# A two-layer diffusion backbone on one core: side streams that take a step of their own before they claim banks or wait in TensorE's queue, and head tiles that leave PSUM inside their loop

## The chip, the cores and the metric

The kernel runs on one core of a Trainium2 chip. The metric is the device time of one execution in microseconds (us). A core has five engines that work at the same time, each through its own list of instructions in a fixed order: PE (TensorE, matrix products; PEld is its loading of weights), DVE (VectorE), ACT (ScalarE), POOL (GpSimd) and SP (which issues DMAs). An instruction that waits for a semaphore holds up everything behind it on its engine. PE writes to PSUM, of which there are eight banks; DVE and ACT read the results out.

## The reference

Two request groups, 128 context tokens and 512 latent tokens, go through two layers that share their weights. A layer norms and modulates its input (model width 1024), projects it to the inputs of four branches and to their gates, runs the branches, gates them, merges them and adds the result to the stream. Cut to what matters here:

```python
kk = kk * lax.rsqrt(jnp.sum(kk * kk, axis=-1, keepdims=True) + 1e-12)
for d, rev in ((0, False), (1, True)):            # RWKV-7 scan, forward and reverse
    w_log = -jax.nn.softplus(-(lp['rw_w0'][d] + wd_t @ lp['rw_w_up'][d])) - 0.5
    decay = heads(jnp.exp(-jnp.exp(w_log)))
    a = heads(jax.nn.sigmoid(lp['rw_a0'][d] + adf @ lp['rw_a_up'][d]))
    k_d = k_h * (1.0 + (a - 1.0) * k_a)
    s_fin, o = wkv_scan(s_init[:, d], r_h, decay, k_d, v_h, kk, a, rev)
    o_sum = o_sum + o
mu = jnp.mean(o_sum, axis=-1, keepdims=True)      # group norm of the scan's output, per head
var = jnp.mean(jnp.square(o_sum - mu), axis=-1, keepdims=True)
on = ((o_sum - mu) * lax.rsqrt(var + GN_EPS)).reshape(B, L, BR_W)
y = on * lp['rw_ln_g'] + lp['rw_ln_b'] + bonus

def rmsnorm(x, g):                                # before each layer and at the end
    return x * lax.rsqrt(jnp.mean(x * x, axis=-1, keepdims=True) + NORM_EPS) * g
```

The other branches are windowed attention with a sink, a mix of tokens within chunks, and a pooling branch. All five outputs (two streams, new keys, new values, new scan states) are float32.

## The kernel before

The 640 tokens stand in the free dimension as two halves of 320 (`HF`); the 1024 channels are eight tiles of 128 partitions (`KT`). Every large product is split into three: activations and weights are kept as a high and a low part in the type fp32r, and PE computes hi times whi, lo times whi and hi times wlo (`m<-hi,whi`, `m<-lo,whi`, `m<-hi,wlo` in the rows below). ACT casts the high part of a weight (`whi<-raw`), DVE subtracts it to get the low part (`wlo<-raw,whi`). There are 7008 such main products of 128x128 by 128x320, 3504 in each layer.

A planner (class `Clock`, from L91) writes the order of each engine once, when the program is built. It runs the main stream, which is the large products, and several **side streams**: attention (`at`), the scan of the RWKV branch, its group norm (`gn0`, `gn1`), the norm of the next layer's input (`normed`) and smaller ones. Each stream is a Python generator. A `yield` in a side stream ends a step: at that point the planner can lay main products between this step and the next, and it looks at its own model of engine times, and from a stream's second step on at its model of PSUM banks, to decide when the next step is due. A `yield` in the main stream with a name waits until a side stream has marked that name. What is written without a `yield` between stands back to back in PE's order, whatever the data behind it does at run time.

PSUM's banks are shared out by name: four `m` banks for main products, two `x` banks for most side products, one `c` and one `o` bank for attention and scan. A bank can be written again when its last result has been read.

Places in the code that the change touches:

- `rstd_thin` (L600) computes the factor of a norm. Six thin products (`x<-cst,t` and `x<-cst,nacc`: two partial sums of squares, three token blocks) go into one `x` bank, ACT takes the square root, DVE the reciprocal (`rst`), and `spread()` transposes the factors over the partitions (`x<-cst,rst`). `normed` (L622) calls both back to back for each half at the end of layer 0.
- `scan` has `decay(d)` (L709 on), whose last products `x<-cst,A` are read by four exponentials on ACT (`A<-x`). For the reverse direction (d = 1) the next step is the **value flip**: the tokens of the values are put in reverse order by a product (`x<-vn,cst`). It writes the banks that those exponentials read.
- `group_norm` (L981) starts with the **centering**: it claims two `x` banks at once and subtracts the head's mean by a product (`x<-yb,cst`).
- `head()` (L1315) computes the first six tiles of layer 0, three tiles in two halves (`ck`, `cv` and a query tile), with the sum over k outermost, into four `m` banks and the `c` and `o` banks. After the loop all six are copied out by `put`, alternately by ACT and DVE, and `put` of a second half marks the tile as ready for attention.

Of the kernel before, what the change touches and what calls it, by code (L numbers as in the profile page):

```python
# [14 lines left out]
P = 128  # L15
NL = 2
D = 1024
KT = D // P
# [3 lines left out]
HF = T // 2  # L22
# [5 lines left out]
HEAD = ["ck", "cv", "q0", "q1"]  # L28
# [267 lines left out]
def hybrid_layers_kernel(ctx: ExitStack, tc: tile.TileContext, xt, cond, condb, wm, wt, wa, wb, wo, pa, pb, pc, gfin, kctx, vctx,  # L296
# [16 lines left out]
    def X():  # L313
        return ck.alloc("x", ps_x.tile([P, 512], F32, tag="x", name="x"), 2)
# [284 lines left out]
    def rstd_thin(acc, more=None):  # L599

        ms = X()
        parts = [acc] if more is None else [acc, more]
        for i, o in enumerate((0, P, HF - P)):
            for x in parts:
                mm(ms[:, 2 * i:2 * i + 2], x[:, o:o + P], K("mean")[:, 0:2], start=i == 0 and x is acc,
                   stop=i == 2 and x is parts[-1])
        st = S([P, 6], "rst", 2)
        A.activation(st, ms[:, 0:6], AF.Sqrt, bias=eps[:, 0:1])
        V.reciprocal(st, st)

        def spread():
            bc = X()
            for i, (o, c) in enumerate(((0, 0), (P, 0), (2 * P, C))):
                mm(bc[:, o:min(o + P, HF)], st[:, 2 * i:2 * i + 1].to_broadcast([P, P]), K("ident")[:, c:P])
            A.copy(acc, bc[:, 0:HF])
            return bc

        return spread

    def normed(xs, accs, l, out, bs, ahead, more=None):  # L620
        rs = {}
        for b in bs:  # L622
            rs[b] = accs[b]
            if l:
                rstd_thin(accs[b], more)()
        for b in bs:
            out[b] = (S([P, KT, HF], f"hi{b}", dt=F32R), S([P, KT, HF], f"lo{b}", dt=F32R))
            ck.mark(f"hh{l}{b}")
        late = []

        def finish(k, ts):
            shift = mods[l][0]
            for b in bs:
                hi, lo = out[b]
                for s, e, g in segs[b]:
                    V.scalar_tensor_tensor(lo[:, k, s:e], ts[b][:, s:e], shift[:, k, g:g + 1], hi[:, k, s:e],
                                           ALU.add, ALU.subtract)
                ck.mark(f"h{l}{b}.{k}")

        for k in range(KT):  # L640
            yield f"mod{l}.{k}"
            shift, gsc = mods[l][0], mods[l][1]
            ts = {b: S([P, HF], "t", 4) for b in bs}
            for b in bs:
                for s, e, g in segs[b]:
                    V.scalar_tensor_tensor(ts[b][:, s:e], xs[b][:, k, s:e], gsc[:, k, g:g + 1], rs[b][:, s:e],
                                           ALU.mult, ALU.mult)
            if ahead and late:
                finish(*late.pop(0))
            for b in bs:  # L650
                for s, e, g in segs[b]:
                    A.activation(out[b][0][:, k, s:e], ts[b][:, s:e], AF.Identity, bias=shift[:, k, g:g + 1])
            late.append((k, ts))
            if not ahead:
                finish(*late.pop(0))
            if k + 1 < KT:
                yield VQ
        for x in late:
            finish(*x)
# [11 lines left out]
    def layer(l, h, prb):  # L671
# [23 lines left out]
        def scan(ft, ta, kt, rt, vt):  # L695
# [89 lines left out]
            for d in range(2):  # L785
                for c0, n in ((0, 8), (8, 2)):
                    px = X()
                    for hh in range(2):
                        r = slice(64 * hh, 64 * hh + 64)
                        if d:  # L790
                            mm(px[r, 0:n * C], K("anti")[r, r], vn[hh][r, c0:c0 + n, :].rearrange("p c s -> p (c s)"))
                            continue
                        for i in range(n):
                            mm(px[r, i * C:(i + 1) * C], vt[r, (c0 + i) * C:(c0 + i + 1) * C], K("ident")[r, r])
                    for hh in range(2):
                        r = slice(64 * hh, 64 * hh + 64)
                        src = px[r, 0:n * C].rearrange("p (c s) -> p c s", s=C)
                        o0 = 2 * NC - c0 - n if d else c0
                        A.copy(vn[hh][r, o0:o0 + n, :], src[:, ::-1, :] if d else src)
                yield  # L800
                yield from keys(d)
                if d == 0:
                    yield from decay(1)
            yield
            for b in range(2):
                px = X()
# [95 lines left out]
            for j in range(8):  # L902
# [12 lines left out]
                for n in lanes:  # L915
                    s = state[n]
                    for d, i in enumerate(at[n]):
                        o = slice(col[n, d], col[n, d] + C)
# [9 lines left out]
                for n in lanes:  # L928
                    for d, i in enumerate(at[n]):
                        o = slice(col[n, d], col[n, d] + C)  # L930
# [50 lines left out]
                state.update(nxt_state)  # L981
                yield
            def group_norm():
                oc = [X(), X()]
                cen = S([P, 2, HF], "v")
                sqs = []
                for b in range(2):
                    mm(oc[b][:, 0:HF], K("cent"), osum[:, hs[b]])
                    V.tensor_copy(cen[:, b], oc[b][:, 0:HF])
                    sq = S([P, HF], "t", 4)  # L990
                    A.activation(sq, oc[b][:, 0:HF], AF.Square)
                    sqs.append(sq)
                yield
                for b in range(2):
                    vr = X()
                    mm(vr[:, 0:HF], K("bones"), sqs[b])
                    rn = S([P, HF], "t", 4)
                    A.activation(rn, vr[:, 0:HF], AF.Sqrt, bias=eps[:, 2:3], scale=1.0 / 64)
                    V.reciprocal(rn, rn)
                    V.scalar_tensor_tensor(cen[:, b], cen[:, b], prm("lng")[:, ft:ft + 1], rn, ALU.mult, ALU.mult)  # L1000
                    V.scalar_tensor_tensor(osum[:, hs[b]], cen[:, b], prm("lnb")[:, ft:ft + 1], bon[:, hs[b]], ALU.add, ALU.add)
                yield
# [312 lines left out]
        def head():  # L1315
# [17 lines left out]
            if l == 0:  # L1333
# [5 lines left out]
                for k in range(KT):  # L1339
                    turn = k % 4 == 3  # L1340
                    for b, i in [(b, i) for i in range(3) for b in range(2)] if turn else [
                            (b, i) for b in range(2) for i in range(3)]:
                        yield f"h{l}{b}.{k}"
                        yield from accum([out[i][b]], ws[i], k % 4, 1, [rhs_h[b]], k, k == 0, k == KT - 1)
                        if turn and b:
                            if k + 1 < KT:
                                ws[i] = piece(0)
                            else:
                                split(nxt[2] + i)
                yield f"n{l}0"  # L1350
                for i in range(3):
                    for b in range(2):
                        put(HEAD[i], b, out[i][b])
                o = yield from main()
                for b in range(2):
                    put(HEAD[3], b, o[b])
# [331 lines left out]
```

## Time and profile before

| | us |
|---|---|
| median of 3 runs | 1394.77 |
| lowest and highest | 1393.83, 1397.92 |
| the profiled execution's own time | 1396.28 |
| its span in the profile | 1394.2 |
| PE busy | 1349.6 (97%) |
| PEld busy | 1259.7 (90%) |
| DVE busy | 925.8 (66%) |
| ACT busy | 565.3 (41%) |
| POOL busy | 48.0 (3%) |

The profile is of one execution. A timeline gives one row to each run of equal instructions: start, length from the first start to the last end, engine, line, operation, tiles, count, and in brackets how long the engine stood idle just before and what released it. Line 331 (`mm`) and 335 (transposes) are helpers for every PE instruction, line 290 for every instruction of the other engines, so instructions are told apart by their tiles. Products overlap: one main product is shown as 0.31 us long while the next starts 0.15 us after it. PEclk is the granted clock of PE as a share of full speed; its mean over the execution was 0.992.

### The profile page before, as it was taken

To read this page: it belongs to the slowest core of one execution; us is meant where nothing else is said; L and a number is where in the kernel's file an instruction comes from. 1 tells how busy PE (TensorE), PEld (TensorE's weight loads), DVE (VectorE), ACT (ScalarE), POOL (GpSimd) and SP (SyncE) were. 2 spreads that over 40 slices of the span, in tenths; PEclk is the share of its full clock that TensorE was granted. 3 is DMA by queue.
4 is the path that set the end of the run, shared out by engine and by line. 5 is a ranking of instruction groups with operands and counts; after the bars stand their busy time and mean duration, and the time that the engine had idled before them with its cause. 6 is when DMAs were issued, how large, how long until landed. Compare 5 with 4: busy or idle time off the path is not lost. (4 is left out here: it accounts for less than half of the span.)

```text
span 1394.2 us, 27698 instructions
## 1 busy us (share of the span) xinstructions
PE 1349.6 (97%) x11350; PEld 1259.7 (90%) x11350; DVE 925.8 (66%) x2056; ACT 565.3 (41%) x1258; POOL 48.0 (3%) x43
## 2 busy tenths in 40 slices
PE   5899999999999999999999999999999999999997
PEld 4889889988999988999999988898799998899997
DVE  5766677856777856658876667694377684464474
ACT  5455622234522333325555555223354233332364
POOL 0100010000000000000001001000000000000000
PEclk9999999999999999999999999999999999999998
DMA  9411133421224331751113212433022323144012
GB/s 376 148 54 61 39 108 106 108 81 66 67 88 115 106 94 63 267 187 61 61 62 120 72 54 66 109 87 88 24 60 65 89 83 82 37 157 156 22 39 76
DMA packets 86503, 132.61 MB, mean 95 GB/s; under 512 B 44744, under 2 KB 46152, under 8 KB 84456
## 3 DMA queue, kind: packets, MB, share of 16 engines
q1 hardware_dynamic: 86376, 130.84, 29.9%
q8 instruction: 89, 1.46, 0.4%
q14 instruction: 38, 0.31, 0.1%
HBM read 120.46 MB, written 10.35 MB: 94 GB/s over the span
## 5 line engine op out<-in xcount | busy, mean ns | idle before, releaser
L331 PE MATMUL m<-hi,whi 128*128 128x320 f32 x2064 | 666.1, 323 | 3.3 <-ACT whi L290 1.6
L331 PE MATMUL m<-hi,wlo 128*128 128x320 f32 x2064 | 641.4, 311 | 1.9 <-DVE wlo L290 1.9
L331 PE MATMUL m<-lo,whi 128*128 128x320 f32 x2064 | 640.6, 310 | 2.0 <-DVE lo L290 1.3
L331 PEld LDWEIGHTS m<-hi,whi 128*128 128x128 f32 x2064 | 389.9, 189 | 25.3 <-issue 10.2
L331 PEld LDWEIGHTS m<-lo,whi 128*128 128x128 f32 x2064 | 390.1, 189 | 5.1 <-DVE lo L290 2.0
L331 PEld LDWEIGHTS m<-hi,wlo 128*128 128x128 f32 x2064 | 389.5, 189 | 4.5 <-DVE wlo L290 4.2
L290 ACT CAST whi<-raw 128x640 fp32r<-128x640 f32 (+1 forms) x220 | 148.9, 682 | 282.3 <-PE m L331 262.6
L290 DVE TENSOR_TENSOR wlo<-raw,whi 128x640 fp32r<-128x640 f32 (+1 forms) x220 | 168.1, 769 | 107.6 <-ACT whi L290 104.8
L290 ACT ACTIVATE t<-m 128x320 f32<-128x320 f32 x152 | 64.2, 434 | 87.3 <-PE m L331 87.1
L290 DVE TENSOR_TENSOR kb<-kb 80x31 f32<-80x31 f32 (+15 forms) x248 | 86.2, 348 | 10.2 <-DMA kb<-ad 3.5
L290 DVE SCALAR_TENSOR_TENSOR t<-t,m 128x320 f32<-128x320 f32 x120 | 57.7, 481 | 47.0 <-PE m L331 38.0
L331 PE MATMUL m<-ysh,whi 128*128 128x320 f32 x256 | 82.6, 323 | 0.7 <-DVE t L290 0.7
L290 DVE CUSTOM_DVE_ANT_0 junk<-wt,sil 128x1024 bf16<-128x1024 f32 x64 | 79.2, 1237 | 3.8 <-DMA wt<-wt 3.6
L331 PE MATMUL m<-ysh,wlo 128*128 128x320 f32 x256 | 79.1, 309 | 0.0
L331 PE MATMUL m<-ysl,whi 128*128 128x320 f32 x256 | 79.0, 309 | 0.0
L290 DVE TENSOR_TENSOR xm<-xm,t 128x320 f32<-128x320 f32 x96 | 50.8, 530 | 3.3
L331 PEld LDWEIGHTS m<-ysh,whi 128*128 128x128 f32 x256 | 48.1, 188 | 3.4 <-DVE t L290 0.9
L331 PEld LDWEIGHTS m<-ysl,whi 128*128 128x128 f32 x256 | 48.2, 188 | 0.2
L331 PEld LDWEIGHTS m<-ysh,wlo 128*128 128x128 f32 x256 | 48.1, 188 | 0.0
L290 DVE RECIPROCAL t<-t 128x320 f32<-128x320 f32 x16 | 34.4, 2149 | 19.1 <-ACT t L290 19.1
L290 ACT ACTIVATE vn<-c 64x128 f32<-64x128 f32 x40 | 10.8, 271 | 79.0 <-DVE vn L290 79.0
L290 DVE TENSOR_TENSOR A<-x,cst 128x512 f32<-128x512 f32 x40 | 25.7, 684 | 20.6 <-PE x L331 20.6
(242 smaller groups left out, 1517.8 us busy)
## 6 DMA issues: line engine op xcount, KB each, us to landing
raw<-wb SPq DMA_DIRECT2D x128, 320.0 KB, 2.9
raw<-wa SPq DMA_DIRECT2D x92, 256.0 KB, 2.9
wt<-wt SPq DMA_DIRECT2D x32, 512.0 KB, 4.0
A<-wm SPq DMA_DIRECT2D x4, 1024.0 KB, 9.1
A<-wo SPq DMA_DIRECT2D x8, 512.0 KB, 6.0
xm<-xt SPq DMA_DIRECT2D x4, 640.0 KB
ad<-A SPq DMA_DIRECT2D x8, 320.0 KB
qr<-wm SPq DMA_DIRECT2D x2, 1024.0 KB
```

Source lines behind the costliest of these rows:

```text
L290: return f(out, *a, **k)
L331: PE.matmul(out, lhsT, rhs, start=start, stop=stop)
```

## The change

Four side steps are cut in two by a `yield`, so that main products can be laid between. In `normed` it stands between the factor of a norm and its spreading; in `scan` between the decay of the reverse direction and the value flip; in `group_norm` before the centering, which thus becomes the stream's second step, at which the planner looks at the banks. In `rstd_thin` the loops are exchanged: the three products of the first sum come first, then the three of the second. In `head()` each of the six tiles is copied out as soon as its last product is issued, within the loop, and no longer after it. No instruction is added or dropped; the planner lays all streams anew.

```diff
@@ rstd_thin
-        for i, o in enumerate((0, P, HF - P)):
-            for x in parts:
+        for x in parts:
+            for i, o in enumerate((0, P, HF - P)):
                 mm(ms[:, 2 * i:2 * i + 2], x[:, o:o + P], K("mean")[:, 0:2], start=i == 0 and x is acc,
                    stop=i == 2 and x is parts[-1])
@@ normed
             if l:
-                rstd_thin(accs[b], more)()
+                spread = rstd_thin(accs[b], more)
+                yield
+                spread()
@@ scan
                 if d == 0:
                     yield from decay(1)
+                    yield
@@ group_norm
             def group_norm():
+                yield
                 oc = [X(), X()]
@@ head
                         yield from accum([out[i][b]], ws[i], k % 4, 1, [rhs_h[b]], k, k == 0, k == KT - 1)
+                        if k == KT - 1:
+                            yield f"n{l}0"
+                            put(HEAD[i], b, out[i][b])
                         if turn and b:
...
-                yield f"n{l}0"
-                for i in range(3):
-                    for b in range(2):
-                        put(HEAD[i], b, out[i][b])
```

DVE's order at the end of the head tiles of layer 0, before. `xm0` holds the key and query tiles, `bon` the value tile, `m_267` and `m_269` are the banks of their second halves; STREAM_SHUFFLE and the two operations on `vn0` and `xm0` turn the key tile by its rotary angles, of which POOL computes one product in between:

```order
L290 TENSOR_TENSOR wlo_610<-raw_482,whi_609 128x512
L290 TENSOR_SCALAR wt_517<-wt_517 128x1024
L290 TENSOR_TENSOR sil_515<-wt_517,sil_515 128x1024
L290 TENSOR_TENSOR wlo_625<-raw_510,whi_624 128x512
L290 TENSOR_TENSOR wlo_637<-raw_525,whi_636 128x512
L290 COPY xm0_642<-m_267 128x320
L290 COPY bon_223<-m_269 128x320
L290 COPY xm0_642<-o_271 128x320
L290 STREAM_SHUFFLE vn0_578<-xm0_642 128x512
L290 TENSOR_TENSOR vn0_578<-vn0_578,xm1_574 128x512
L290 TENSOR_TENSOR xm0_642<-xm0_642,vn0_578 128x512
```

The same rows of DVE after:

```order
L290 COPY xm0_606<-m_267 128x320
L290 TENSOR_TENSOR wlo_614<-raw_482,whi_613 128x512
L290 TENSOR_SCALAR wt_517<-wt_517 128x1024
L290 TENSOR_TENSOR sil_515<-wt_517,sil_515 128x1024
L290 STREAM_SHUFFLE vn0_578<-xm0_606 128x512
L290 TENSOR_TENSOR vn0_578<-vn0_578,xm1_574 128x512
L290 TENSOR_TENSOR xm0_606<-xm0_606,vn0_578 128x512
L290 COPY bon_223<-m_269 128x320
L290 TENSOR_TENSOR wlo_636<-raw_510,whi_635 128x512
L290 COPY xm0_606<-o_271 128x320
L290 TENSOR_TENSOR wlo_650<-raw_525,whi_649 128x512
```

The copy of the key tile moves ahead of a weight split, the rotation of the key tile moves ahead of the copy of the value tile `bon`, and two weight splits move behind it.

PE's order at the value flip of layer 1, before. `x<-cst,A` are the last products of the decay, `x<-vn,cst` the flip, `o<-cst,kbt` and `c<-cst,kbt` transposes of attention's weights:

```order
L335 MATMUL o<-cst,kbt 128x128 x4
L335 MATMUL c<-cst,kbt 128x128 x4
L331 MATMUL x<-cst,A_8445 128x128 x5
L331 MATMUL x<-vn_8446,cst 64x512
L331 MATMUL x<-vn_8447,cst 64x512
L331 MATMUL x<-vn_8446,cst 64x128
L331 MATMUL x<-vn_8447,cst 64x128
L335 MATMUL o<-cst,kbt 128x128 x2
L331 MATMUL m<-hi_7571,whi 128x320
L331 MATMUL m<-lo_7572,whi 128x320
```

The end of the same stretch after. `x<-cst,A` stands twelve main products ahead of the first transpose shown here:

```order
L331 MATMUL m<-hi_7580,whi 128x320
L331 MATMUL m<-lo_7581,whi 128x320
L331 MATMUL m<-hi_7580,wlo 128x320
L335 MATMUL o<-cst,kbt 128x128 x2
L331 MATMUL m<-hi_7971,whi 128x320
L331 MATMUL m<-lo_7972,whi 128x320
L331 MATMUL m<-hi_7971,wlo 128x320
L331 MATMUL x<-vn_8455,cst 64x512
L331 MATMUL x<-vn_8456,cst 64x512
L331 MATMUL x<-vn_8455,cst 64x128
L331 MATMUL x<-vn_8456,cst 64x128
```

The flip no longer follows `x<-cst,A` directly: fifteen main products and two transposes stand between. The centering moves in the same manner, fifteen main products behind the `x<-adt,pb` that it followed, and the spreading of the factors six main products behind the thin products.

PE's order at the end of attention in layer 1, before. `o<-y,xm` is the last product of values with the transposed weights:

```order
L335 MATMUL o<-cst,kbt 128x128 x4
L335 MATMUL c<-cst,kbt 128x128 x4
L331 MATMUL m<-hi_7571,whi 128x320
L331 MATMUL m<-lo_7572,whi 128x320
L331 MATMUL m<-hi_7571,wlo 128x320
L331 MATMUL m<-hi_7953,whi 128x320
L331 MATMUL m<-lo_7954,whi 128x320
L331 MATMUL m<-hi_7953,wlo 128x320
L331 MATMUL m<-hi_7571,whi 128x320
L331 MATMUL m<-lo_7572,whi 128x320
L331 MATMUL m<-hi_7571,wlo 128x320
L331 MATMUL o<-y,xm_8152 64x128 x8
```

And after:

```order
L331 MATMUL m<-lo_7972,whi 128x320
L331 MATMUL m<-hi_7971,wlo 128x320
L335 MATMUL o<-cst,kbt 128x128 x4
L335 MATMUL c<-cst,kbt 128x128 x4
L331 MATMUL o<-y,xm_8157 64x128 x8
L331 MATMUL m<-hi_7580,whi 128x320
```

Here nine main products that stood between the transposes and the last product of values are gone from that place; the three rows follow one another.

## Rows read from the trace of the kernel before

**Rows 1.** The page, section 1: busy time and share of the span by engine.

```profile
PE 1349.6 (97%) x11350; PEld 1259.7 (90%) x11350; DVE 925.8 (66%) x2056; ACT 565.3 (41%) x1258; POOL 48.0 (3%) x43
```

**Rows 2.** Waits of PE: engine line waited for: total, times, longest.

```profile
PE x L331 <- DVE nacc L290: 12.0, 2, 10.9
PE x L331 <- ACT A L290: 4.9, 6, 1.4
PE x L331 <- DVE rst L290: 2.5, 4, 0.7
```

**Rows 3.** Timeline of PE, value flip in layer 1: start, length, instruction, [idle before].

```profile
845.83 1.28 PE L331 MATMUL x<-cst,A 128*128 128x128 f32 x10
848.50 1.41 PE L331 MATMUL x<-vn,cst 64*64 64x512 f32 x8 [1.39 <-ACT A L290]
```

**Rows 4.** Timeline of ACT over the same flip.

```profile
848.03 1.40 ACT L290 ACTIVATE A<-x 128x128 f32<-128x128 f32 x4
849.63 1.72 ACT L290 COPY vn<-x 64x512 f32<-64x512 f32 x4 [0.20 <-PE x L331]
```

**Rows 5.** Timeline of PE, first centering of layer 1.

```profile
1003.23 1.34 PE L331 MATMUL x<-adt,pb 64*128 64x320 f32 x4
1004.65 0.81 PE L331 MATMUL x<-yb,cst 128*128 128x320 f32 x2
1006.35 1.32 PE L331 MATMUL x<-yb,cst 128*128 128x320 f32 x2 [0.89 <-ACT A L290]
1007.00 0.94 PE L331 MATMUL m<-hi,whi 128*128 128x320 f32 x1
```

**Rows 6.** Timeline of PE, second centering of layer 1.

```profile
1213.28 1.24 PE L331 MATMUL x<-yb,cst 128*128 128x320 f32 x4
1214.12 0.55 PE L331 MATMUL m<-ysh,whi 128*128 128x320 f32 x1
```

**Rows 7.** Timeline of PE, the spreading of both halves' factors before layer 1.

```profile
678.74 0.88 PE L331 MATMUL x<-cst,rst 128*128 128x128 f32 x6 [0.58 <-DVE rst L290]
...
711.56 0.85 PE L331 MATMUL x<-cst,rst 128*128 128x128 f32 x6 [0.68 <-DVE rst L290]
```

**Rows 8.** Stretches: us, each engine's busy time, PEclk, DMA share, GB/s.

```profile
712.96:716.36 3.40, 3.40 (x15) 3.40 (x14) 1.64 (x4) 1.56 (x4) 0.00 (x0) 0.50 0.74 258
1006.50:1009.90 3.40, 3.40 (x12) 3.01 (x13) 0.49 (x1) 3.02 (x5) 0.00 (x0) 0.50 0.00 0
```

**Rows 9.** Timeline of PE and of DVE, head tiles of layer 0.

```profile
59.57 0.41 PE L331 MATMUL m<-hi,whi 128*128 128x320 f32 x1 [1.44 <-ACT xm L290]
...
62.21 0.55 PE L335 MATMUL x<-cst,bon 128*128 128x128 f32 x3 [0.84 <-DVE bon L290]
...
60.06 1.29 DVE L290 TENSOR_TENSOR wlo<-raw,whi 128x512 fp32r<-128x512 f32 x2
...
61.67 0.48 DVE L290 COPY bon<-m 128x320 f32<-128x320 f32 x1
...
62.47 0.74 DVE L290 STREAM_SHUFFLE vn<-xm 128x512 f32<-128x512 f32 x1
...
65.13 0.69 DVE L290 TENSOR_TENSOR xm<-xm,vn 128x512 f32<-128x512 f32 x1 [1.19 <-POOL xm L290]
...
65.75 0.74 DVE L290 STREAM_SHUFFLE vn<-xm 128x512 f32<-128x512 f32 x1
```

**Rows 10.** Timeline of DVE and of PE, end of attention in layer 1.

```profile
854.39 0.69 DVE L290 COPY y<-c 128x512 f32<-128x512 f32 x1 [0.24 <-PE c L335]
...
854.11 0.39 PE L331 MATMUL m<-hi,whi 128*128 128x320 f32 x1
854.33 0.31 PE L331 MATMUL m<-lo,whi 128*128 128x320 f32 x1
854.48 0.31 PE L331 MATMUL m<-hi,wlo 128*128 128x320 f32 x1
```

**Rows 11.** Timeline of PE, a bank taken back in the third merge of layer 1.

```profile
1225.06 0.41 PE L331 MATMUL m<-ysh,whi 128*128 128x320 f32 x1 [0.66 <-DVE t L290]
```

## The prediction

> **What bounds the kernel now.** I read the page's busy times first, then the waits of PE, then the timeline of PE around each place that the diff names, with ACT or DVE beside it, and last the granted clock in stretches. PE is busy for 97% of the span [rows 1], so a microsecond that another engine saves counts only where PE stands still for it. The waits say where: 12.0 us for `nacc`, of which 10.9 us is one wait at the start that the change does not reach; 4.9 us for `A` in six waits; 2.5 us for `rst` in four, of which two belong to the final norm and stay [rows 2]. The change can therefore win single waits of about 1 us and no more. The question is how many, what each costs besides the idle time shown, and what new waits the new order makes.
>
> Idle time understates a wait. Main products are 0.31 us long and start 0.15 us apart [rows 10], so the last one before a wait runs out for 0.16 us in which the next would already have started. I add 0.16 us to each wait that goes.
>
> [...] By the idle times alone the sum below would be some 2.5 us smaller.
>
> **The value flip.** In the first scan of layer 1 the products `x<-cst,A` start at 845.83 and the flip at 848.50, after 1.39 us idle [rows 3]. It waits for exponentials on ACT that read its banks and that run at 848.03, behind the softmax's exponentials [rows 4]. Layer 0 shows the same 1.39 us, and the second scans 0.17 us each; with the two centerings below these make the 4.9 us in six waits: 2 x 1.39 + 2 x 0.17 + 2 x 0.89 [rows 2]. The new order puts 36, 15, 12 and 12 main products between (layer 0, layer 1, then the second scans). Fifteen are 15 x 0.15 = 2.25 us, more than 1.39 + 0.16 = 1.55. So the waits go: 2 x 1.55 + 2 x 0.33 = 3.8 us. The centering below, where both ends can be read, costs 0.2 to 0.45 us more than idle plus 0.16; with 0.45 on the two long waits it would be 4.7. I take 4.3, between the two, with 3.1 (idle alone) and 4.7 as bounds. In layer 1 the attention step behind the flip needs the flip's banks, which ACT empties with four copies of 1.72 us together [rows 4]; main products cover most of that, and I charge 0.25 us.
>
> **The centering.** It waits 0.89 us in layer 1, for the last exponentials of the decay, which read the two banks that it claims [rows 5]; layer 0 shows the same 0.89 us. From `x<-adt,pb` at 1003.23 to the next main product at 1007.00 are 3.77 us [rows 5]. The products before the centering take 1.42 us of it (1003.23 to 1004.65), and a centering that does not wait takes 0.84 us from its start to the next main product [rows 6]. So the wait costs 3.77 - 1.42 - 0.84 = 1.5 us in layer 1 and by the same reckoning 1.25 us in layer 0. The new order puts fifteen main products (2.25 us) between: -2.8 us. Bounds: -1.8 (idle alone) and -3.4.
>
> **The factors.** The spreading waits 0.58 us for the first half and 0.68 us for the second [rows 7]. The new order puts six main products between, 6 x 0.15 = 0.9 us, more than 0.58 + 0.16 = 0.74 or 0.84. Both waits go: -1.6 us, bounds -1.3 (idle alone) and -1.8. The exchanged order of the thin products costs and gives nothing, since PE waits for none of their results but `rst`, which comes after the last of them in either order.
>
> **The clock.** [...] In 712.96 to 716.36 PE starts only 15 products in 3.40 us, in 1006.50 to 1009.90 only 12 [rows 8]; 3.40 / 0.15 would be 23. Each stretch loses about 8 to 11 products, 1.2 to 1.6 us. They begin 1.4 us after the wait for the second factors ends at 711.56 [rows 7] and 0.15 us after that of the centering ends at 1006.35 [rows 5], both waits that this change removes. If they follow from those waits they go: -2.8 us. But side products of few columns stand there as well and stay. I give it one half: -1.4 us, bounds 0 and -2.8.
>
> **The head tiles of layer 0.** Today main products wait 1.44 us at 59.57 for ACT to empty the first `m` bank, and the transposes of `bon` wait 0.84 us at 62.21 for DVE's copy [rows 9]. With the copies in the loop the first bank is free in time: -1.6 us. The second wait grows. DVE's copy of `bon` now stands behind the key tile's rotation, which lasts from 62.47 to 65.75, 3.28 us, with DVE held up for 1.19 us by POOL [rows 9]. The new order has on DVE one weight split, the two modulation operations, then that rotation, then `bon`. Today the two modulation operations end at 60.06, when the next split starts [rows 9]. So `bon` starts at 60.06 + 3.28 = 63.34 and ends, 0.48 us later, at 63.8. Today PE is ready for the waiting transposes at 62.21 - 0.84 = 61.4. They come fifteen main products later now, and 1.6 us are saved ahead: 61.4 + 2.25 - 1.6 = 62.0. So they wait 1.8 us, 1.0 us more than today. Sum: -0.6 us, bounds -2.4 (both waits go, if the copy comes earlier than I reckon) and +1.5 (the first wait stays, the second grows).
>
> [...] The trace of before kept the full clock here with a wait of 0.84 us. [...]
>
> **What is late next.** At the end of attention in layer 1 the last product of values now follows its transposes directly. Today the second transposes run until main products start at 854.11, and DVE's copy of them takes from 854.39 to 855.08 [rows 10]; nine main products cover that. Uncovered it is up to 855.08 - 854.11 = 0.97 us; I take +0.7, bounds +0.4 and +1.0. In the third merge of layer 1 a main product waits 0.66 us for a bank that DVE empties behind the group norm's reciprocals [rows 11]; the group norm falls elsewhere now: -0.4, bounds -0.9 and +0.7. In layer 0 nearly every side step between the head tiles and the first merge stands at another place, and over the whole program PE's order has eleven runs of side products more. New small waits are as likely there as the going of old ones, and each new run is one more place for them. By the nearest row, 0.66 us [rows 11], one or two of them are +1.0; bounds -1 and +3.
>
> **Sum.** -4.3 + 0.25 - 2.8 - 1.6 - 1.4 - 0.6 + 0.7 - 0.4 + 1.0 = -9.15 us. The profiled execution took 1396.28 us (its span is 1394.2, the rest lies around it and stays), so 1387.1. The median shown is 1.51 us below that execution: 1385.6.
>
> **Rivals.** 0.3% of this time, 4.2 us, is about what a measurement can tell from no change: faster means below 1390.6, slower above 1399.0.
>
> *The waits only change place.* The flip and the centering stop waiting, but their banks are then held longer, so that attention and the mix, which use the same two `x` banks, wait instead; the head tiles cost +1.5 and the small waits +3. For it: ACT is the releaser in most places, and its queue holds the same work. Against it: ACT is busy for less than half of the span. It leaves -4.3 + 0.25 - 2.8 - 1.6 + 1.5 + 0.7 + 3 = -2.95, and about 1 us more for the waits of attention and mix, -1.95: 1392.8.
>
> *Only the drained waits count.* The idle time of the flip, the centering and the factors goes (3.1 + 1.8 + 1.3 = 6.2 us), the clock falls where it fell, and the rest adds 0.25 + 0.7 + 1.0 - 0.4 - 0.6 = 0.95: -5.25, 1389.5. For it: at the second scans PE's waits are small and it is not seen what they cost beyond their idle time.
>
> *The clock falls at the head tiles too.* All terms as in the sum, but the two stretches of [rows 8] stay (+1.4) and the wait of 1.8 us before the transposes, longer than any that they follow, brings a third (+1.4): -6.35, 1388.4.
>
> *The second scan of layer 1 comes too late (slower).* The planner puts the second centering of layer 1 48 main products (7.2 us) later than before. From it to the third merge's bank the chain takes 1213.28 to 1225.06, 11.8 us [rows 6, 11], and in the new order 132 main products, 19.8 us, stand between it and the first product that needs its result. If the scan's own chain on DVE and ACT runs later than planned, the first 8.0 us are free and each microsecond beyond them is a microsecond of idle PE. It must be 8.0 + 9.15 = 17.2 us late to eat the gain and 21.4 us to be slower by 4.2: 1399.0. Against it: the list of waits shows no wait of more than 1.4 us after the start [rows 2], so the plan has been kept well.
>
> *More comes back.* Both clock stretches go and the head tiles lose both waits: -9.15 - 1.4 - 1.8 = -12.35, 1382.4.
>
> **How the numbers follow.** Forecast 0.48, only the drained waits 0.12, clock at the head tiles 0.10, waits change place 0.18, second scan late 0.06, more comes back 0.06. Faster holds the forecast, the two rivals below 1390.6 and the last: 0.76, of which I move 0.02 to "same" since 1389.5 lies near the edge: 0.74. Same 0.20, slower 0.06. The range 1381.0 to 1393.5 takes in all but the late scan and the outer ends of the others.
>
> **What would show it.** Right: no idle time of PE in front of `x<-vn,cst`, the first `x<-yb,cst` of each layer and the `x<-cst,rst` between the layers; no wait for `xm` at the first product after the head tiles; a wait of about 1.8 us for `bon` there; a new wait of 0.4 to 1 us before the last `o<-y,xm` of attention in layer 1; one or two stretches at half clock fewer. Wrong: a wait for `bon` under 1 us or over 3; a wait of over 1 us at a product that had none; half clock after the head tiles; or a sum of PE's waits lower by 6 us with a time that has not moved.

## The result and the profile after

The changed kernel takes 1388.47 us (median of 5 runs, 1383.34 to 1389.26); before, in 5 runs of the same series, it was 1396.31 us (1393.83 to 1397.92). The ratio is 0.994 with a 95% interval of 0.9919 to 0.9962: faster by 0.4 to 0.8%. The forecast was 1385.6 us in a range of 1381.0 to 1393.5. The profiled execution took 1388.71 us against 1396.28, 7.6 us less, where the sum had said 9.15. By the interval the gain is 5.3 to 11.3 us.

The page's first section, against [rows 1]:

```profile
PE 1349.5 (97%) x11350; PEld 1261.6 (91%) x11350; DVE 926.3 (67%) x2056; ACT 566.2 (41%) x1258; POOL 51.7 (4%) x43
```

PE is busy for 1349.5 us, 0.1 us less, in a span that is 7.3 us shorter, so what the span lost is idle time of PE. The waits of PE (total, times, longest), against [rows 2]:

```profile
PE x L331 <- DVE nacc L290: 12.0, 2, 10.9
PE m L331 <- DVE wlo L290: 2.6, 7, 1.0
PE x L335 <- DVE bon L290: 1.7, 1, 1.7
...
PE x L331 <- DVE rst L290: 1.3, 2, 0.7
PE o L331 <- DVE y L290: 1.0, 1, 1.0
```

The row for `A` of [rows 2], 4.9 us in six waits, is gone; `rst` is down to the final norm's two. In their place stand waits for `bon` (1.7 us), for `y` (1.0 us) and a longer total for `wlo`. The one for `y` is in attention of layer 0: a product `o<-y,xm` at 130.20, which did not wait before, waits 1.01 us for DVE's copy of the transposed weights, which stands behind two operations `kb<-A` of the scan, 0.81 us each. Now the places, in the order of the prediction. The value flip of layer 1 in PE's timeline, against [rows 3]:

```profile
836.98 1.28 PE L331 MATMUL x<-cst,A 128*128 128x128 f32 x10
...
840.60 1.29 PE L331 MATMUL x<-vn,cst 64*64 64x512 f32 x8
```

The flip starts 3.6 us behind `x<-cst,A`, with main products and attention's transposes between, and no idle time ahead of it. The head tiles of layer 0, DVE and then PE, against [rows 9]:

```profile
60.50 0.70 DVE L290 TENSOR_SCALAR wt<-wt 128x1024 f32<-128x1024 f32 x1 [0.27 <-ACT wt L290]
...
62.38 0.73 DVE L290 STREAM_SHUFFLE vn<-xm 128x512 f32<-128x512 f32 x1
...
65.01 0.69 DVE L290 TENSOR_TENSOR xm<-xm,vn 128x512 f32<-128x512 f32 x1 [1.17 <-POOL xm L290]
65.62 0.48 DVE L290 COPY bon<-m 128x320 f32<-128x320 f32 x1
```

```profile
64.06 0.38 PE L335 MATMUL x<-cst,bon 128*128 128x128 f32 x2
66.16 0.55 PE L335 MATMUL x<-cst,bon 128*128 128x128 f32 x3 [1.71 <-DVE bon L290]
```

DVE's copy of `bon` starts at 65.62, right behind the rotation that POOL holds up, and the transposes wait 1.71 us. The wait for `xm` is gone. The end of attention in layer 1, against [rows 10]:

```profile
854.68 0.60 PE L335 MATMUL c<-cst,kbt 128*128 128x128 f32 x4
855.51 1.20 PE L331 MATMUL o<-y,xm 128*64 128x128 f32 x16 [0.24 <-ACT y L290]
856.65 0.41 PE L331 MATMUL m<-hi,whi 128*128 128x320 f32 x1
```

The run from 854.68 to the next main product takes 1.97 us. Its 4 transposes and 16 products take 0.36 and 1.03 us where nothing holds them, so the uncovered copies cost 0.6 us, though only 0.24 us shows as idle time. The norm between the layers, PE's timeline and the stretch at half clock, against [rows 7, 8]:

```profile
706.90 0.42 PE L331 MATMUL m<-hi,wlo 128*128 128x320 f32 x1 [0.97 <-DVE wlo L290]
...
708.61 1.12 PE L331 MATMUL x<-cst,t 128*128 128x2 f32 x6
...
711.33 1.38 PE L331 MATMUL x<-cst,rst 128*128 128x128 f32 x6
```

```profile
708.95:715.78 6.83, 6.83 (x29) 6.83 (x29) 4.40 (x10) 3.28 (x7) 0.00 (x0) 0.50 0.95 336
```

The spreading at 711.33 no longer waits for `rst`. But a main product waits 0.97 us for a low weight part at 706.90, which no row of before showed there, and the half clock (PEclk 0.50) now lasts 6.8 us, where it lasted 3.4.

To see where the time went I take the start of certain main products in PE's timeline, which have the same number in every kernel (the first has number 0): the 96th (in the head tiles of layer 0), the 2064th and 2640th (merges of layer 0), the 3800th (in the head tiles of layer 1, behind the norm) and the 5568th (merge of layer 1). The table has the lengths of before and the differences to them, in us, each from one profiled execution, and the ratios of the timed runs; the other kernels are the experiments below.

| | ratio to before (95% interval) | to 96 | 96-2064 | 2064-2640 | 2640-3800 | 3800-5568 | 5568 to end |
|---|---|---|---|---|---|---|---|
| before | | 50.9 | 409.8 | 114.1 | 186.4 | 374.6 | 258.4 |
| changed kernel | 0.994 (0.9919-0.9962) | +2.6 | -3.8 | -1.0 | +0.9 | -3.8 | -2.2 |
| flip alone | 1.0061 (1.0047-1.0075) | +0.5 | -0.4 | +1.9 | +2.6 | +4.7 | -2.6 |
| centering alone | 1.003 (1.002-1.0041) | +0.1 | -1.8 | +3.4 | +1.6 | +0.7 | -0.1 |
| factors alone | 0.9968 (0.9957-0.9979) | +1.7 | -0.3 | -0.3 | -2.1 | -0.3 | -0.4 |
| head alone | 1.0027 (1.0016-1.0037) | +3.6 | -4.4 | -1.0 | +3.6 | +4.8 | -1.1 |
| without head | 0.9969 (0.9957-0.9981) | +1.3 | -4.0 | +3.6 | -1.6 | -2.7 | -1.6 |
| without factors | 1.0003 (0.9992-1.0015) | +0.1 | -3.7 | -1.0 | +3.1 | +0.3 | -2.2 |
| without flip | 0.9983 (0.9972-0.9994) | +2.1 | -1.1 | -0.6 | -2.1 | +2.1 | -1.7 |
| without centering | 1.0019 (1.0009-1.003) | +1.5 | -2.5 | -1.0 | +3.3 | +2.6 | -0.7 |
| without flip, longer load | 0.9924 (0.9912-0.9937) | +2.1 | -4.5 | -0.6 | -0.6 | -5.0 | -1.5 |
| changed, longer load | 0.9996 (0.9987-1.0005) | +1.7 | -3.8 | -1.0 | +2.3 | +1.2 | -0.7 |
| changed, `bon` first | 1.0014 (1.0003-1.0025) | +1.9 | -2.2 | +1.3 | +2.3 | -1.3 | -2.6 |
| both | 0.9978 (0.9966-0.9989) | +1.8 | -5.7 | +6.0 | -0.7 | -2.7 | -0.2 |

The changed kernel loses 2.6 us before the 96th product, in the norm at the start, where nothing of the change is. There 16 narrow products took 1.94 us at 20.11, where 16 of the same shape took 1.07 at 20.40 before, and the stretch at half clock that begins near 26 lasts 6.8 us instead of 3.4. PE's order up to the 96th product is the same in all fourteen kernels and the column still varies by 3.6 us, so it belongs to the single execution. Behind it the two traces differ by 9.9 us. The two stretches with flip and centering give 3.8 us each.

### The profile page after: what moved, and what is told of

Read it like the earlier page. It is cut to its first block, busy times and chain, and to the rows that moved or that the text cites. A ratio compares the mean times of both kernels' runs of the same rounds, so it can differ in the third digit from the quotient of the medians.

```text
span 1386.9 us, 27713 instructions
## 1 busy us (share of the span) xinstructions
PE 1349.5 (97%) x11350; PEld 1261.6 (91%) x11350; DVE 926.3 (67%) x2056; ACT 566.2 (41%) x1258; POOL 51.7 (4%) x43
## 3 DMA queue, kind: packets, MB, share of 16 engines
q8 instruction: 89, 1.46, 0.4%
## 4 chain that ended last, share of the span: by engine, by line
PE 84%; issue 6%; DVE 5%; ACT 3%; POOL 1%; DMA 1%; SPq 0%; POOLq 0%; DVEq 0%; ACTq 0%
PE m L331 65%; PE x L331 10%; PE c L331 5%; PE o L331 2%; DVE wlo L290 2%; ACT whi L290 1%; DVE t L290 1%; PE x L335 1%; DMA A<-wm 1%; PE o L335 1%; PE c L335 0%; ACT vn L290 0%; DVE kb L290 0%; ACT hi L290 0%; POOL xm L290 0%
## 5 line engine op out<-in xcount | busy, mean ns | idle before, releaser
L290 DVE TENSOR_TENSOR wlo<-raw,whi 128x640 fp32r<-128x640 f32 (+1 forms) x220 | 171.9, 784 | 108.5 <-ACT whi L290 104.8
L290 DVE CUSTOM_DVE_ANT_0 kbt<-x,xm 128x512 f32<-128x512 f32 (+3 forms) x56 | 26.8, 516 | 21.4 <-PE x L331 21.4
```

The costliest lines, as they stand in the source:

```text
L290: return f(out, *a, **k)
```

## The experiments

**One edit at a time, on the kernel before.** Each of the first four kernels has one hunk of the diff.

```diff
                     yield from decay(1)
+                    yield
```

> The kernel before with the step before the value flip alone. My theory (a wait that goes is worth its idle time plus the time that the last product runs out): PE's four waits for A before x<-vn,cst, 3.1 us of idle time, go, nothing of their size comes in their place, and the time falls by 4.3 us (3.1 to 4.7). Rival (waits only change place): the four waits go but new waits of over 1.5 us together appear at attention or the mix, and the time falls by less than 2 us. The waits before the centering (2 x 0.89) and before the factors (0.58, 0.68) stay in both. Clock: the half-clock stretches near 713 and 1006 stay if they follow from the waits of the factors and of the centering.

It took 1405.37 us against 1397.34: 8 us slower, where both theories had a gain. The four waits before the flip are gone, as both said. PE's timeline of the flip alone in layer 1:

```profile
893.80 2.27 PE L331 MATMUL x<-qr,kb 64*128 64x128 f32 x16 [2.14 <-DVE y L290]
896.66 1.43 PE L331 MATMUL x<-t,pb 128*128 128x320 f32 x2 [0.59 <-DVE A L290]
...
899.77 1.43 PE L331 MATMUL x<-t,pb 128*128 128x320 f32 x2 [0.83 <-DVE t L290]
```

The last score step of the scan (`x<-qr,kb`) and the pooling branch (`x<-t,pb`) now run into each other: 2.14 us for DVE's `y`, then 0.59 and 0.83 us, and the clock is at half for 10 us from 893.8 on. Another 4.5 us are lost at 2064-3800, with a wait of 1.43 us for `wlo` at 569.94 and a second stretch at half clock, at 682. The rival was nearer, but both were wrong on the sign. The wait before the centering of layer 1 stands as before, 0.89 us at 1018.4, and no half clock follows it.

```diff
             def group_norm():
+                yield
                 oc = [X(), X()]
```

> The kernel before with the step before the centering alone. My theory: the two waits of 0.89 us go, the time falls by 2.8 us, and by up to 1.6 us more if the half-clock stretch near 1006, which begins 0.15 us after that wait, follows from it. Rival (idle time alone counts): -1.8 us. Rival (the centering only comes later and the second scan behind it too): no gain, the wait reappears behind it, at the product that needs the group norm.

1401.39 us, 4 us slower. The two waits of 0.89 us and the half clock near 1006 are gone; the stretch 96-2064 gains 1.8 us. DVE and then PE in layer 1:

```profile
907.80 0.19 DVE L290 TENSOR_TENSOR kb<-kb 80x31 f32<-80x31 f32 x1 [3.24 <-DMA kb<-ad]
```

```profile
917.12 0.78 PE L331 MATMUL x<-t,pb 128*128 128x320 f32 x2 [2.75 <-DVE t L290]
```

DVE stands still for 3.24 us for a load `kb<-ad`, part of the scan's round trip through DRAM. Behind it in DVE's queue stands the pooling branch, and PE waits 2.75 us for that. The larger loss, 3.4 us, is at 2064-2640: PE waits 2.52 us at 559.78 for `t`, the squares of the second group norm of layer 0, and the clock is at half for 3.4 us there. That is the third expectation's mechanism, but at a product of the group norm itself. At its own place the edit gave what was reckoned: from the 1290th to the 1500th product, with the same products in both, PE takes 1.6 us less, of which 0.3 us is another wait, so 1.3 us for the centering of layer 0.

```diff
-                rstd_thin(accs[b], more)()
+                spread = rstd_thin(accs[b], more)
+                yield
+                spread()
```

> The kernel before with the step between factor and spreading alone, and the exchanged order of the thin products. In the changed kernel both waits for rst between the layers are gone, but a wait of 0.97 us for a low weight part (wlo) stands at 706.9 instead and the half-clock stretch there is 6.8 us long instead of 3.4. Theory 1 (the step itself shifts DVE's order, and the wait for wlo is its price): the 0.97 us wait is here too, and the time falls by less than 0.6 us. Theory 2 (that wait comes from the other edits): no new wait of over 0.3 us, -1.6 us. Clock: if the stretch follows from the wait for rst it is gone here; if it follows from the thin products themselves it stays.

1392.97 us, 4.4 us faster, the only edit that gains alone. The wait of 0.96 us for `wlo` is here too (theory 1), yet the stretch 2640-3800 is 2.1 us shorter, and the half clock there is gone. So the wait is the step's price, and theory 1's sum was wrong, by the clock among other things: behind the 96th product the trace is 3.4 us shorter.

```diff
+                        if k == KT - 1:
+                            yield f"n{l}0"
+                            put(HEAD[i], b, out[i][b])
```

> The kernel before with the copies of the head tiles in their loop alone. My theory: the wait of 1.44 us for xm goes, the wait for bon before the transposes grows from 0.84 to 1.7 to 1.8 us because DVE's copy of bon stands behind the key tile's rotation with its product on POOL, and the stretch from the 96th to the 912th main product gains 0.6 us at most. Rival: the copies in the loop take DVE from the weight splits, new waits for wlo appear, and the time is 1 to 2 us longer. Rival: the whole gain of layer 0 in the changed kernel beyond flip and centering (about 0.4 us) comes from here.

1399.78 us, 2.4 us slower (3.8 by the ratio). At the place itself it is as expected: no wait for `xm`, 1.72 us for `bon`. But from the 96th to the 912th product 2.7 us are gained, not 0.6 at most, the stretch 96-2064 gains 4.4 us, and PE's four waits at the flips are 0.17 us each, 0.7 us in all and no longer 3.1, although the flip's step is not in this kernel: its products now come at a point where the exponentials on ACT are not behind a softmax. Layer 1 loses more; PE's timeline there:

```profile
860.52 2.41 PE L331 MATMUL x<-bon,cst 128*128 128x320 f32 x4 [2.67 <-DVE bon L290]
```

The products of the scan's bonus wait 2.67 us for DVE, whose queue had the softmax's and the weights' work ahead of `bon`. Here, too, DVE waits for the load `kb<-ad`, and PE waits 1.73 us at `x<-t,pb` behind it, at 921.5. DVE:

```profile
904.05 2.74 DVE L290 TENSOR_TENSOR kb<-kb 80x31 f32<-80x31 f32 x10 [3.16 <-DMA kb<-ad]
```

**One edit left out.** The next four are the changed kernel with one of those hunks undone.

> The changed kernel with the head tiles' copies put back behind their loop (flip, centering and factors stay). By my sum the head is worth 0.6 us: the time is 0 to 1 us above that of the changed kernel, 7 us below before, with waits of 1.2 to 1.4 us for xm and 0.85 us for bon back and the wait of 1.7 us gone. Rival (layout): the four edits do not add, as the flip alone cost 8 us, the centering alone 4 and the head alone 2.4: then this kernel lies anywhere from 10 us faster to 8 us slower than before, with new waits of 1 us and more in layer 1, at the pooling branch's x<-t,pb or at the bonus x<-bon,cst, for results of DVE.

1391.82 us, 4.3 us below before and 4 us slower than the changed kernel by the ratios, where the sum said 0 to 1. That is nearer the rival, though the long new wait is in layer 0. The waits for `xm` (1.16 us) and `bon` (0.84 us) are back. The stretch 96-2064 is as short as with the head edit; 3.6 us are lost against before at 2064-2640, where one main product waits and 3.4 us at half clock follow:

```profile
567.33 0.42 PE L331 MATMUL m<-hi,wlo 128*128 128x320 f32 x1 [2.05 <-DVE wlo L290]
```

> The changed kernel with factor and spreading back to back again (flip, centering and head stay). The factors alone gave 4.4 us, of which 2.1 us lie in the stretch from the 3300th to the 3800th main product and the rest in layer 1 behind it. Theory (layout of layer 1): the same place moves what follows in layer 1, so the loss here is more than the 0.6 us of its own waits: 2 to 6 us slower than the changed kernel, with new waits behind the 3800th main product. Rival (terms add): 0.3 to 1 us slower than the changed kernel.

1397.69 us, as before the change and 8.8 us slower than the changed kernel by the ratios, more than both expectations. Against the changed kernel the trace loses 4.1 us at 3800-5568 (new waits of 1.93, 0.59 and 1.29 us at `x<-qr,kb` and `x<-t,pb`; one of 1.23 us at `x<-t,pb` stands in the changed kernel too) and 2.2 us at the norm. The profiled execution, 1392.47 us at a mean clock of 0.993, is 5 us below the median, whose runs have about 0.989; so part of the loss is probably half clock, which this trace does not show.

> The changed kernel without the step before the value flip. Terms add: the four waits for A come back (3.1 us idle), 4 us slower than the changed kernel. Layout: the flip's own step is what moved the second scan and the pooling branch in the flip-alone kernel, where it cost 8 us in all; then this kernel is not slower than the changed one by 4 us, and its waits at x<-t,pb and x<-bon in layer 1 differ from those of the changed kernel by more than 1 us together.

1394.47 us, 6 us slower than the changed kernel by the ratios, more than the terms say. But the waits at the flip hardly come back: three stand there, of 0.37, 0.17 and 0.17 us. The loss is elsewhere, as the layout expectation had it, whose bound of 4 us does not hold either. DVE, then PE, in layer 1:

```profile
898.07 1.31 DVE L290 TENSOR_TENSOR wlo<-raw,whi 128x512 fp32r<-128x512 f32 x1 [1.04 <-ACT whi L290]
902.74 0.41 DVE L290 TENSOR_TENSOR kb<-kb 80x31 f32<-80x31 f32 x2 [3.36 <-DMA kb<-ad]
903.07 0.85 DVE L290 TENSOR_TENSOR xm<-xm 128x680 f32<-128x680 f32 x1
...
909.06 1.39 DVE L290 SCALAR_TENSOR_TENSOR t<-xm 64x128 f32<-64x128 f32 x4
```

```profile
910.60 1.40 PE L331 MATMUL x<-t,pb 128*128 128x320 f32 x2 [3.88 <-DVE t L290]
```

Again DVE waits for `kb<-ad`, 3.36 us. The pooling branch (`xm`, `t`) stands behind it and PE waits 3.88 us.

> The changed kernel without the step before the centering. Terms add: the two waits of 0.89 us come back, 2.8 us slower than the changed kernel (4.4 if the half-clock stretch near 1006 comes back with them). Layout: differs from that by more than 2 us either way, with a wait of over 1 us at a product that had none in the changed kernel.

1398.9 us, 11 us slower than the changed kernel by the ratios. The waits are back as they were, without the half clock that had followed them:

```profile
1010.11 0.81 PE L331 MATMUL x<-yb,cst 128*128 128x320 f32 x2 [0.89 <-ACT A L290]
```

With the same wait in layer 0 that is 1.8 us. The rest, as the layout expectation had it, comes with waits at `x<-qr,kb` (1.61 us), `x<-t,pb` (0.58 and 2.07 us, where the changed kernel has one of 1.24), `x<-cst,A` (1.29 and 1.46 us) and, behind the norm, for `lo` (1.53 us).

**The planner told of a longer load.** If DVE is held by a step that it starts before its load is there, the planner's number for that load should decide it. Only that number is changed; the transfer is the same.

```diff
-                    "h n s t -> (h n) s t"), True, 8)
+                    "h n s t -> (h n) s t"), True, 20)
```

> The changed kernel without the flip's step, in which the planner reckons 2.7 us more for the two loads kb<-ad of the scan's round trip through DRAM (a number in its table; the DMAs are the same). Without it DVE stood 3.36 us idle at kb<-kb for that load, with the pooling branch behind it, and PE waited 3.88 us at x<-t,pb near 910. Theory (a side step that DVE starts too early holds up what stands behind it in its queue, and that is what made the single edits slow): DVE's idle time for kb<-ad in layer 1 falls below 1 us, PE's wait of 3.88 us falls below 1.5 us, and the time falls by 2 to 5 us. Rival (the wait at x<-t,pb comes from the pooling branch's own chain): DVE no longer waits for kb<-ad, but PE still waits over 2.5 us there and the time stays within 1.5 us.

1385.98 us: 8 us faster than without the edit, and the fastest of all kernels here (ratio to before 0.9924; the changed kernel's interval overlaps it). DVE and PE at the same place:

```profile
897.71 0.85 DVE L290 TENSOR_TENSOR xm<-xm 128x680 f32<-128x680 f32 x1
...
902.03 0.40 DVE L290 TENSOR_TENSOR kb<-kb 80x31 f32<-80x31 f32 x2
...
903.18 1.39 DVE L290 SCALAR_TENSOR_TENSOR t<-xm 64x128 f32<-64x128 f32 x4
```

```profile
905.66 0.70 PE L331 MATMUL x<-t,pb 128*128 128x320 f32 x2
```

`kb` comes behind `xm`, its load has landed, and neither engine waits. The theory holds at its place: 3.36 us and 3.88 us become nothing, the 6.8 us at half clock near 909 go with them, and 3800-5568 is 7.1 us shorter. The whole gain is larger than the 2 to 5 us expected. Elsewhere the new order moves the time too: 96-2064 is 3.4 us shorter (a wait of 2.17 us at `x<-cst,A` shrank to 1.01 us and a stretch at half clock near 383 went), 2640-3800 is 1.5 us longer.

> The changed kernel with the same 2.7 us more for the two loads in the planner's reckoning. In its trace DVE does not wait for this load between 890 and 930, so by the theory little is to be won there: within 2 us of the changed kernel (7.8 us below before), the waits for kb<-ad in layer 0 shorter. Rival (every new lay of the side steps moves the time by several us): 3 us or more away from the changed kernel, with other waits.

1396.2 us, 7.8 us slower than the changed kernel by the ratios: the rival. Layer 0 is the same to 0.1 us, although DVE's wait of 2.14 us for the load at 436 is gone: no wait of PE had hung on it. Layer 1 is laid anew and falls into the collision of the flip alone, with half clock behind it:

```profile
887.68 1.35 PE L331 MATMUL x<-qr,kb 64*128 64x128 f32 x16 [1.61 <-DVE y L290]
...
892.95 1.41 PE L331 MATMUL x<-t,pb 128*128 128x320 f32 x2 [1.04 <-DVE t L290]
```

```profile
889.32:896.15 6.83, 5.49 (x17) 4.12 (x18) 4.00 (x8) 1.49 (x5) 0.00 (x0) 0.50 0.45 96
```

**The copy of the value tile first.**

```diff
                 evac(target(n, b), o)
-                if b:
+                if b and (l or n != HEAD[0]):
                     ck.mark(L + n)
+                    if not l and n == HEAD[1]:
+                        ck.mark(L + HEAD[0])
```

> The changed kernel, in which the key tile of layer 0 is marked as ready only when the value tile has been copied out, so that DVE's copy of bon stands ahead of the rotation and its product on POOL. Theory (the wait of 1.7 us for bon at 66.16 is the copy's place in DVE's queue): that wait falls below 0.5 us. If nothing else moves, the time falls by 1.5 us. Rival (layout): the wait goes but the time moves by 3 us or more either way, with waits of over 1 us elsewhere.

1398.41 us. The wait is gone, DVE and PE at the head tiles:

```profile
61.71 0.48 DVE L290 COPY bon<-m 128x320 f32<-128x320 f32 x1
...
63.72 0.73 DVE L290 STREAM_SHUFFLE vn<-xm 128x512 f32<-128x512 f32 x1
```

```profile
62.53 0.71 PE L335 MATMUL x<-cst,bon 128*128 128x128 f32 x5
```

But the time is 10 us longer than that of the changed kernel: the rival. The trace, of an execution 2.7 us below the median, loses against that kernel in every stretch from the 96th to the 5568th product; among the new waits is one for the bonus of layer 1:

```profile
862.79 1.34 PE L331 MATMUL x<-bon,cst 128*128 128x320 f32 x4 [1.80 <-DVE bon L290]
```

> Both edits on the changed kernel, the value tile's copy first and 2.7 us more for the two loads. Terms add: 1.5 to 3 us faster than the changed kernel, some 10 us below before. Layout: anywhere within 8 us of before; if the single long waits (over 1.5 us after the first 30 us) are what makes the difference between the lays, the time goes with their sum.

1394.19 us: the two edits, 7.8 and 10 us slower each than the changed kernel, are together 5.3 us slower. Nothing adds. They meet at 2064-2640, with waits of 1.37, 1.91 and 1.19 us and two stretches at half clock. Long waits do not order the kernels by themselves: of those over 1.5 us, the expectation's measure, the changed kernel and the fastest have 1.7 us each behind the 96th product and the kernel before has none.

## Why the prediction was right, and where it was not

*Which waits go.* Right at every place: no wait for `A` at flips and centerings, none for `rst` between the layers, none for `xm`. This is the part of the mechanism that was right.

*The head tiles.* A wait of 1.8 us was forecast from DVE's new order and the durations of before; it is 1.71 us. Both of its ends, PE at the transposes and the end of `bon`, come 2.3 to 2.5 us later than reckoned, as all of this execution does there. PE kept the full clock behind the wait of 1.71 us (PEclk 1.00 from 64 to 72), in this kernel and in the six others that have it.

*The end of attention and the group norm.* +0.7 forecast, 0.6 measured, though as idle time only 0.24 us shows, less than the 0.4 to 1 us that was to be seen. The wait of 1.01 us at `o<-y,xm` in layer 0 was not foreseen. It comes with the head edit (0.99 us with the head alone) and by the forecast's own list, a wait of over 1 us at a product that had none, it is a sign of being wrong; the +1.0 us for new small waits covers its size. The bank's wait in the third merge went from 0.66 to 0.47 us and that of layer 0 (0.26 us) is gone, but two waits of the same kind, 0.27 and 0.23 us, stand at other places: about nothing where 0.4 us was forecast.

*The factors.* -1.6 forecast for the waits; the stretch 2640-3800 is 0.9 us longer. The waits went, but a wait of 0.97 us for `wlo` came, which the step brings with it (it is in the factors alone as well), and the half clock doubled. The order of PE had been read here, that of DVE not.

*The clock.* One stretch of two was to go. Near 1006 it went, near 713 it stayed and grew from 3.4 to 6.8 us, at the start it grew by as much and near 1355 one of 3.4 us went that the forecast had left; PEclk was 0.50 in each. That the wait in front decides it is refuted. Behind the wait of 0.89 us before the centering of layer 1 the clock falls in the kernel before and with the factors alone; with the flip alone, the head alone and without the centering's step the same wait stands and the full clock stays. Near 713 the full clock stays with the head alone, which has both waits for `rst`, and falls in the changed kernel, which has neither. What decides it stays open.

*The sum.* This step is right in its result, 9.15 forecast against 7.6 us, and not in its reasoning. It took each wait as the property of the step that waits. Alone, the four edits moved the median by +8.0, +4.1, -4.4 and +2.4 us, +10.1 together; the whole moved it by -7.8. Left out, they cost 4.0 (head), 8.8 (factors), 6.0 (flip) and 11.0 us (centering) by the ratios, 30 together. The flip's waits show why: the head edit alone takes them from 3.1 to 0.7 us, and undoing the flip's step in the changed kernel brings back no more than 0.7. Each edit lays all later side steps anew, and kernels that differ in one edit lie up to 11 us apart, in layer 1 above all: the stretch 3800-5568 alone spans 10 us over these kernels. The forecast had +1.0 us, from -1 to +3, for it. The change came out near the sum because its lay has no wait of over 1.3 us in that stretch, as before had none of over 1.4. That was not foreseen: that the sum came so near is in good part luck, and a range of 1381 to 1393.5 was narrow for an effect of that size.

*What makes a lay bad.* Shown in one pair: DVE takes a step whose load the planner expects too early, and everything behind it waits (without the flip, with and without the longer load). A wait of DVE of over 3 us for this load stands in the centering alone and the head alone too. In the flip alone, without factors, without centering and in the changed kernel with the longer load it is a second pattern, the last score steps against the pooling branch on DVE. In these four the first scan of layer 1 is laid later than in the other ten: 4152 main products stand ahead of its flip and 4269 ahead of the products of its bonus, elsewhere 4140 and 4206 at most. The second pattern was seen in four traces and not tested by itself. The seven kernels with one of the two patterns are the seven whose stretch 3800-5568 is longer than before's, by 0.3 to 4.8 us in one execution each; in the changed kernel and the five others it is shorter.

*The rivals.* The time alone does not tell the forecast from two of them: the gain of 5.3 to 11.3 us holds 9.15 and the 6.35 of "the clock falls at the head tiles too", and comes within 0.1 us of the 5.25 of "only the drained waits count". The first of these two named 1388.4, but its third stretch at half clock is not there: no run shows the 1.4 us that it charges for one behind the head tiles, and in the changed kernel PEclk is 1.00 from 33.1 to 708.9. The second scan of layer 1 is not late: the wait for the third merge's bank is 0.47 us. "The waits only change place" describes the single edits better than the whole, though not by its mechanism: the new waits shown are for DVE and a load, not for banks. Its sum was added wrongly: the terms give -3.25 and not -2.95, and with 1 us more -2.25, which is 1392.5.

## What to carry to other kernels

Where a planner or scheduler lays out the whole program, a wait that an edit removes is its local effect only. Before such waits are summed, see how far the rest of the order moves, and give the range the size of that move. An edit from which little is expected shows it: the longer load on the changed kernel was reckoned at 2 us at most and cost 7.8. When one edit of several is credited with a gain, undo it alone and look whether the waits come back, and look in the queue of the engine that releases PE for a step that waits for a load.

## What the runs showed of the hardware

The load `kb<-ad` was there for DVE 6.7 us after its first issue at 896.04 (without the flip, DVE's row at 902.74), and its two issues took 3.4 us of SP's queue; DVE, in the order that the planner had made for a shorter load, had been ready for it 3.36 us before. SP's row of the two issues:

```profile
896.04 3.42 SPq L327 DMA_DIRECT2D kb<-ad  x2
```

PE's granted clock fell to 0.50 at other places in nearly every one of these kernels, between no time (`bon` first, mean clock of the execution 0.996) and five times (centering alone, 0.989) from the 96th product to the last main product. No wait was found that it always follows: of the five kernels with the wait of 0.89 us before the centering of layer 1 it fell behind it in two.
